# Two-layer diffusion backbone with gated DeltaNet: a pool of its own for the keys of heads 2 and 3, and the condition vectors loaded first

## The chip, the cores and the metric

The kernel runs on one core of one Trainium2 chip. The time is device microseconds of one launch, compared by the median over runs. Engines are named as in the profile: PE (TensorE), DVE (VectorE), ACT (ScalarE), POOL (GpSimd), SP (SyncE, which issues the DMAs).

## The reference, cut to what matters

Two layers, each with a mixing part and a ConvFFN, over 128 context tokens and 1024 latent tokens with 1024 features. The mixing part projects the normalized input once and gives its columns to three groups; the kernel treats the 1152 tokens together, as 9 tiles of 128.

```python
def mixing(h, lp, ctx):
    (a_val, a_gate, q_b, k_b, v_b, z_b, beta_raw, decay_raw,
     q_c, k_c, v_c) = split_projection(h @ lp['w_in'])
    o_a = conformer_conv(a_val, a_gate, ...)          # u = a_val * sigmoid(a_gate); depthwise conv width 31; LayerNorm; silu
    o_b, s_f, s_b = gated_deltanet(q_b, k_b, v_b, z_b, beta_raw, decay_raw, ...)
    o_c = neighbourhood_attention(q_c, k_c, v_c, ...) # or context_attention for the context tokens
    return jnp.concatenate([o_a, o_b, o_c], axis=-1) @ lp['w_out']
```

In `gated_deltanet` q, k and v go through a convolution of width 3 and a silu, and there are 4 heads. Each head is worked in chunks, forward and backward:

```python
    lmat = jnp.where(strict, jnp.einsum('bhnid,bhnjd->bhnij', kb, k) * decay, 0.0)
    sol = lax.linalg.triangular_solve(jnp.eye(CHUNK) + lmat, rhs, lower=True, unit_diagonal=True)
    ...
    s_final, o = lax.scan(step, s0, xs)               # one step for each chunk, a state of 128x128
```

`lmat` needs only k, beta and the decays. The condition vectors enter as `silu(cvec) @ w_ada + b_ada`; the decays of DeltaNet start from `exp(a_log)`.

## The kernel before

All matrix products of the projections are made of three products of high and low parts (L429 to L431, `mm3`), so that float32 precision is kept. A weight block of 128 columns is loaded as `raw` (two buffers), ACT makes `whi`, POOL makes `wlo = raw - whi` (L420). With it `dense` makes one step of 24 matmuls for each of three token blocks (384, 384, 385 columns).

In each layer the DeltaNet heads come in two pairs:

1. Heads 0 and 1: `gdn_dense` makes q, k, v. `preps` makes `lmat` for both, and `invert` (L1617) inverts all its 32x32 diagonal blocks at once, 72 blocks on 72 partitions: a load `F<-fd`, 30 pairs of DVE operations (L1627, L1628) of which each needs the one before, a store `fy<-F`. `gdn_blocks` loads the result back (`room<-fy`), transposes it (L813) and multiplies the blocks up to the full inverse on PE (L820, many small matmuls).
2. `gdn_scan`: the recurrence over the tiles for heads 0 and 1 (L930 to L970; its DVE rows write `ty`).
3. The list `STEPS` = k2, k3, c, q2, e, q3, e, v2, e, v, v3 orders what the program writes next. k2 and k3 are the keys of heads 2 and 3 (`gdn_piece` with `keep`: they stay in SBUF). c is the conformer's dense steps: gate and value blocks, with the DVE product `thg` of both. e is the next stage of `early`: first `gdn_early` for head 2, then for head 3 (turned keys, k·k products, `lmat`), then a second `invert`. v is the conformer's convolution (`conf_conv`): 8 chunks of 292 or 291 columns with 31 DVE operations each on `cu`, 248 a layer. The first `NCV` = 3 chunks are written at the step v, the other 5 (L1712) where the second pair's blocks are written.
4. Output of heads 0 and 1 (`z_dense`, `gdn_out`), then blocks and scan of heads 2 and 3, then attention, the output projection and the ConvFFN.

The order on each engine is not that of the program's text there: a scheduler with priorities sets it (`high_priority(-LOW)` puts the convolution behind, `high_priority(-LOWI)` the second inversion), from dependencies and a model of durations. An order written out by hand rules only the start, attention and the end of the FFN. So a buffer that comes free late moves all that hangs on it.

The buffers in question: pool `r0` (left side) holds `vT` of heads 0 and 1 and the 2880-column tile `F`/`room` of their inversion and blocks; it is given back after the blocks of heads 0 and 1. Pool `r2` comes later on the same side, so it takes the space that `r0` gives back. The tile `e` of `early` lies in `r2`: 3 x 1152 columns for the keys of heads 2 and 3 and for `DA`, and 256 for `kc`. A second `e` holds `F` and the temporary of the second inversion.

Of the kernel before, what the change touches and what calls it, by code (L numbers as in the profile page):

```python
# [9 lines left out]
F32 = mybir.dt.float32  # L10
# [10 lines left out]
KT = 8  # L21
NLAT = 1024
NT = 9
NTOK = 1152
# [19 lines left out]
FB = 2  # L44
ECOLS = 3 * NTOK + 256
NCV = 3
# [62 lines left out]
class K:  # L109
# [23 lines left out]
    def setup(self):  # L133
# [29 lines left out]
        o = VEC["ln_g"][0]  # L163
        nc.vector.tensor_scalar(out=self.hln, in0=vec[:, :, o:o + 4], scalar1=0.5, scalar2=None, op0=ALU.mult)
        self.al = cp.tile([128, L, 2, 2, H], F32, name="al")
        for l in range(L):
            for r in range(2):
                nc.sync.dma_start(out=self.al[:, l, :, r, :], in_=I["adt"][l:l + 1, :, r, :].to_broadcast([128, 2, H]))
            self.act(self.al[:, l, 0], self.al[:, l, 0], AF.Exp)
        cv = cp.tile([128, KT, 2], F32, name="cv")  # L170
        nc.sync.dma_start(out=cv, in_=I["cvec"])
        self.cs = cp.tile([128, KT, 2], F32, name="cs")
        self.act(self.cs, cv, AF.Silu)

# [493 lines left out]

    def gdn_early(self, l, h, S, pool, e, fd):

        nc = self.nc
        i = h - 2
        k = e[:, NTOK * i:NTOK * i + NTOK]
        DA = e[:, 2 * NTOK:3 * NTOK].rearrange("p (m f) -> p m f", f=128)
        kc = e[:, 3 * NTOK:ECOLS]
        nc.sync.dma_start(out=DA, in_=self.dec[i][1])
# [924 lines left out]

    def early(self, l, S, pool, rp):

        fd = self.dp.tile([72, 2, 32, 32], F32, tag="fd", name="fd", bufs=2)
        es = []
        e = rp.tile([128, ECOLS], F32, tag="e", name="e", bufs=1)
        yield e
        for h in (2, 3):
            es.append(self.gdn_early(l, h, S, pool, e, fd[:, h - 2]))
            yield  # L1610
        e = rp.tile([128, ECOLS], F32, tag="e", name="e", bufs=1)
        F = e[0:72, 0:2048].rearrange("p (i a b) -> p i a b", i=2, a=32)
        with self.tc.high_priority(-LOWI):
            w = self.invert(fd, F, e[0:72, 2048:])
        self.es = [(*x, w[:, i]) for i, x in enumerate(es)]
# [17 lines left out]
    def run(self):  # L1633
# [23 lines left out]
        for l in range(L):  # L1657
# [8 lines left out]
            with P("r0") as rp:  # L1666
                ds = [self.gdn_dense(l, h, hh, gc, hp[h], rp) for h in range(2)]
                for h in (2, 3):
                    E, tmp = (hp[h - 2].tile([128, NT, 128], F32, tag=t, name="E", bufs=1) for t in ("XN", "ktm"))
                    self.decays(h, S, E, tmp)  # L1670
                    nc.sync.dma_start(out=self.dec[h - 2][1], in_=E)
                heads = self.preps(l, ds, S, gc, hp, rp)
            sc = left.enter_context(P("scan"))
            o01 = self.gdn_scan(l, heads, S, sc)
            pcp = left.enter_context(P("pconv"))
            with P("r2") as rp:
                ea = self.early(l, S, gc, rp)
                ek = next(ea)
                for step in STEPS:
                    if step == "c":  # L1680
                        self.conf_dense(l, hh, gc)
                    elif step == "e":
                        next(ea, None)
                    elif step == "v":
                        with self.tc.high_priority(-LOW):
                            self.conf_conv(l, range(NCV), pcp)
                    else:
                        h = int(step[1])
                        keep = ek[:, NTOK * (h - 2):NTOK * (h - 1)] if step[0] == "k" else None
                        self.gdn_piece(l, h, "kqv".index(step[0]), hh, gc, keep)  # L1690
            for (h, X, _), o in zip(heads, o01):
                run(self.z_dense(l, h, hh, gc))
# [167 lines left out]
```

## Time and profile before

| | |
|---|---|
| median of 3 runs | 3556.93 us (3555.36 to 3557.3) |
| profiled execution | 3560.4 us |
| its span | 3558.6 us |
| busy: PE, DVE, ACT, POOL | 90%, 59%, 37%, 32% of the span |
| layer 0, first L813 / second L813 | 267.71 / 576.56 us |
| layer 1, first L813 / second L813 | 2056.77 / 2367.87 us |

Durations come from the profiled execution. In a timeline each row has its start and its duration in us, an "x" with the number of like instructions in a row, and in brackets how long the engine was idle ahead of it and what ended that. A window's row gives how long each engine was busy in that stretch; PEclk is the granted clock of TensorE as a share of its upper level (1.0 is 2.4 GHz, 0.5 is 1.2 GHz).

### The profile page before, as it was taken

The page shows a single profiled execution, that of the slowest core. Times are in us where ns is not written, and L with a number is a line of the kernel's source. Part 1 is how long each engine was busy: PE and PEld are TensorE (multiplying, and loading weights), DVE is VectorE, ACT ScalarE, POOL GpSimd, SP SyncE. Part 2 cuts the span into 40 slices and gives each one's busy share as a digit, 9 for nine tenths or more (in the row PEclk, how much of TensorE's full clock was granted, in tenths as well). Part 3 has the DMA queues.
Part 4 walks back from the last instruction along what each step waited for, and adds up shares of the span by engine and source line. Part 5 has one row for each costly group of instructions (what it writes and reads, how often), then busy time and mean ns, then how long its engine had stood idle before and what let it go on. Part 6 is the DMA issues. An engine that isn't in the chain of part 4 may idle for free.

```text
span 3558.6 us, 51089 instructions
## 1 busy us (share of the span) xinstructions
PE 3194.8 (90%) x19072; PEld 2883.6 (81%) x19072; DVE 2104.6 (59%) x3952; ACT 1327.9 (37%) x2988; POOL 1137.9 (32%) x1125
## 2 busy tenths in 40 slices
PE   7857888889999999999988668888799999999997
PEld 4857876755899988989978668787578999999997
DVE  3566896453566566656476758985644444444446
ACT  4425233463543333333254252335644222322223
POOL 2413312523444344434244132225333111221114
PEclk9988989999999999999999879898899999999999
DMA  5410353346423222222144113533452111111113
GB/s 184 113 50 28 112 171 116 94 125 196 133 86 97 70 78 86 81 69 78 42 137 128 42 38 100 160 110 79 127 166 85 41 36 39 45 53 43 36 36 130
DMA packets 243086, 323.79 MB, mean 91 GB/s; under 512 B 76175, under 2 KB 169631, under 8 KB 241750
## 3 DMA queue, kind: packets, MB, share of 16 engines
q1 hardware_dynamic: 242838, 320.52, 29.5%
q8 instruction: 151, 2.47, 0.3%
q14 instruction: 97, 0.79, 0.1%
HBM read 252.85 MB, written 67.59 MB: 90 GB/s over the span
## 4 chain that ended last, share of the span: by engine, by line
PE 58%; DVE 8%; DMA 3%; POOL 3%; ACT 2%; issue 2%; SPq 1%; DVEq 0%; POOLq 0%; ACTq 0%
PE d L429 17%; PE d L431 17%; PE d L430 17%; DVE cu L119 2%; DVE cv L119 1%; PE a L930 1%; POOL wlo L420 1%; PE d L600 1%; DVE adacc L119 1%; PE b L273 1%; POOL adacc L223 1%; DVE F L1628 0%; PE a L820 0%; PE a L387 0%; DVE XN L1627 0%
## 5 line engine op out<-in xcount | busy, mean ns | idle before, releaser
L431 PE MATMUL d<-hhi,wlo 128*128 128x386 f32 (+1 forms) x3072 | 1054.7, 343 | 17.5 <-POOL wlo L420 17.5
L429 PE MATMUL d<-hhi,whi 128*128 128x386 f32 (+1 forms) x3072 | 1051.7, 342 | 13.6 <-DVE cv L119 12.0
L430 PE MATMUL d<-hlo,whi 128*128 128x386 f32 (+1 forms) x3072 | 1051.5, 342 | 0.0
L420 POOL TENSOR_TENSOR wlo<-raw,whi 128x1024 fp32r<-128x1024 f32 x136 | 362.3, 2665 | 1112.2 <-ACT whi L116 1110.5
L429 PEld LDWEIGHTS d<-hhi,whi 128*128 128x128 f32 x3072 | 584.9, 190 | 19.3 <-issue 14.6
L431 PEld LDWEIGHTS d<-hhi,wlo 128*128 128x128 f32 x3072 | 583.0, 190 | 20.3 <-POOL wlo L420 19.1
L119 DVE SCALAR_TENSOR_TENSOR cv<-d,fvec,cv 128x384 f32<-128x384 f32 (+1 forms) x528 | 325.2, 617 | 463.6 <-ACT cv L116 455.1
L430 PEld LDWEIGHTS d<-hlo,whi 128*128 128x128 f32 x3072 | 585.2, 191 | 2.2 <-issue 0.7
L1539 DVE TENSOR_TENSOR f<-d,f 128x512 f32<-128x512 f32 x360 | 244.9, 686 | 164.2 <-PE d L431 162.3
L116 ACT ACTIVATE cv<-d,fvec 128x384 f32<-128x384 f32 (+1 forms) x264 | 174.7, 663 | 440.9 <-PE d L431 432.6
L429 PE MATMUL d<-wdh,ahi 128*128 128x512 f32 x792 | 315.6, 398 | 11.2 <-DVE f L1539 8.8
L430 PE MATMUL d<-wdl,ahi 128*128 128x512 f32 x792 | 313.4, 396 | 0.0
L431 PE MATMUL d<-wdh,alo 128*128 128x512 f32 x792 | 312.5, 395 | 0.0
L119 DVE SCALAR_TENSOR_TENSOR cu<-cu,vec 128x292 f32<-128x292 f32 (+1 forms) x480 | 257.3, 568 | 4.2
L116 ACT ACTIVATE whi<-raw 128x1024 fp32r<-128x1024 f32 x136 | 143.9, 1058 | 197.6 <-PE d L430 127.9
L223 POOL TENSOR_TENSOR adacc<-adacc,adpr 128x512 f32<-128x512 f32 x112 | 152.9, 1365 | 125.5 <-ACT adpr L116 97.5
L429 PEld LDWEIGHTS d<-wdh,ahi 128*128 128x128 f32 x792 | 148.9, 188 | 50.4 <-DVE f L1539 13.4
L431 PEld LDWEIGHTS d<-wdh,alo 128*128 128x128 f32 x792 | 148.7, 188 | 36.2 <-issue 0.7
L430 PEld LDWEIGHTS d<-wdl,ahi 128*128 128x128 f32 x792 | 148.8, 188 | 34.4 <-issue 1.4
L1526 POOL TENSOR_TENSOR wdl<-rawd,wdh 128x512 fp32r<-128x512 f32 x88 | 118.4, 1345 | 181.7 <-ACT wdh L116 181.1
L116 ACT ACTIVATE adpr<-adraw,cs 128x512 f32<-128x512 f32 x112 | 81.0, 723 | 240.0 <-POOL adacc L223 191.6
L1515 DVE TENSOR_TENSOR alo<-sg,ahi 128x384 fp32r<-128x384 f32 x132 | 111.9, 848 | 70.0 <-ACT ahi L116 69.8
(381 smaller groups left out, 5202.4 us busy)
## 6 DMA issues: line engine op xcount, KB each, us to landing
raw<-in_w_up_t SPq DMA_DIRECT2D x88, 512.0 KB
adraw<-in_w_ada SPq DMA_DIRECT2D x112, 256.0 KB
raw<-in_w_in_t SPq DMA_DIRECT2D x48, 512.0 KB
rawd<-in_w_down SPq DMA_DIRECT2D x88, 256.0 KB
xs<-x SPq DMA_DIRECT2D x27, 512.0 KB
x<-xs SPq DMA_DIRECT2D x27, 512.0 KB
rawa<-in_w_ada SPq DMA_DIRECT2D x24, 512.0 KB
x<-in_x SPq DMA_DIRECT2D x18, 512.0 KB
```

What stands on the lines that cost most here:

```text
L116: return self.nc.scalar.activation(out=out, in_=in_, func=func, **kw)
L119: return self.nc.vector.scalar_tensor_tensor(out=out, in0=in0, scalar=s, in1=in1, op0=op0, op1=op1, **kw)
L223: nc.gpsimd.tensor_tensor(out=acc[:, 1, :], in0=acc[:, 1, :], in1=pr, op=ALU.add)
L273: nc.tensor.matmul(ps[0:2, :], self.cs[:, k, :], r[:, 512 * i:512 * i + 512], start=(k == 0), stop=False)
L420: nc.gpsimd.tensor_tensor(out=lo[:, :n], in0=raw[:, :n], in1=hi[:, :n].bitcast(F32), op=ALU.subtract)
L429: nc.tensor.matmul(out, shi, mhi, start=(i == 0), stop=False)
L430: nc.tensor.matmul(out, shi, mlo, start=False, stop=False)
L431: nc.tensor.matmul(out, slo, mhi, start=False, stop=(i == n - 1))
L600: nc.tensor.matmul(ps[:, :NBC[b]], w[:, k, :], x[:, k, :NBC[b]], start=(k == 0 and i == 0), stop=(k == KT - 1 and i == 2))
L1515: nc.vector.tensor_tensor(out=lo[:, :n], in0=sg[:, :n], in1=hi[:, :n].bitcast(F32), op=ALU.subtract)
L1526: nc.gpsimd.tensor_tensor(out=lo, in0=raw[:, :512], in1=hi[:].bitcast(F32), op=ALU.subtract)
L1539: nc.vector.tensor_tensor(out=f[t][:, cs], in0=ps, in1=f[t][:, cs], op=ALU.add)
```

## The change

The keys of heads 2 and 3 get a tile `keys` of 2 x 1152 columns in a pool `keys` on the right side, opened when `r0` is closed in the program's text, and closed behind `r2`. The tile `e` shrinks to 1152 + 256 columns for `DA` and `kc` and is allocated once. The second inversion takes `F` from `keys` (the keys are used up by then) and its temporary from `e`. In `setup` the load of the condition vectors and their silu come ahead of the loads and exponentials of the decay factors.

```diff
-ECOLS = 3 * NTOK + 256
+ECOLS = NTOK + 256
...
+        cv = cp.tile([128, KT, 2], F32, name="cv")
+        nc.sync.dma_start(out=cv, in_=I["cvec"])
+        self.cs = cp.tile([128, KT, 2], F32, name="cs")
+        self.act(self.cs, cv, AF.Silu)
         self.al = cp.tile([128, L, 2, 2, H], F32, name="al")
...
-        cv = cp.tile([128, KT, 2], F32, name="cv")
-        nc.sync.dma_start(out=cv, in_=I["cvec"])
-        self.cs = cp.tile([128, KT, 2], F32, name="cs")
-        self.act(self.cs, cv, AF.Silu)
...
-    def gdn_early(self, l, h, S, pool, e, fd):
+    def gdn_early(self, l, h, S, pool, keys, e, fd):
...
-        k = e[:, NTOK * i:NTOK * i + NTOK]
-        DA = e[:, 2 * NTOK:3 * NTOK].rearrange("p (m f) -> p m f", f=128)
-        kc = e[:, 3 * NTOK:ECOLS]
+        k = keys[:, NTOK * i:NTOK * i + NTOK]
+        DA = e[:, 0:NTOK].rearrange("p (m f) -> p m f", f=128)
+        kc = e[:, NTOK:ECOLS]
...
-    def early(self, l, S, pool, rp):
+    def early(self, l, S, pool, keys, rp):
...
         e = rp.tile([128, ECOLS], F32, tag="e", name="e", bufs=1)
-        yield e
         for h in (2, 3):
-            es.append(self.gdn_early(l, h, S, pool, e, fd[:, h - 2]))
+            es.append(self.gdn_early(l, h, S, pool, keys, e, fd[:, h - 2]))
             yield
-        e = rp.tile([128, ECOLS], F32, tag="e", name="e", bufs=1)
-        F = e[0:72, 0:2048].rearrange("p (i a b) -> p i a b", i=2, a=32)
+        F = keys[0:72, 0:2048].rearrange("p (i a b) -> p i a b", i=2, a=32)
         with self.tc.high_priority(-LOWI):
-            w = self.invert(fd, F, e[0:72, 2048:])
+            w = self.invert(fd, F, e[0:72])
...
+            ks = ExitStack()
+            keys = ks.enter_context(R("keys")).tile([128, 2 * NTOK], F32, name="keys", bufs=1)
             sc = left.enter_context(P("scan"))
...
-                        keep = ek[:, NTOK * (h - 2):NTOK * (h - 1)] if step[0] == "k" else None
+                        keep = keys[:, NTOK * (h - 2):NTOK * (h - 1)] if step[0] == "k" else None
...
+            ks.close()
```

PE, layer 0, before: around the first block product (names: d is the accumulator of a dense step, a that of the blocks).

```order
L430 MATMUL d_3086<-hlo_144,whi_3082 128x386
L431 MATMUL d_3086<-hhi_143,wlo_3083 128x386
L820 MATMUL a_1864<-room_1821,DA_1557 32x32 x36
L820 MATMUL a_1902<-room_1821,DA_1601 32x32 x2
L820 MATMUL a_1940<-room_1821 32x32 x25
L820 MATMUL a_1902<-room_1821,DA_1601 32x32 x34
L820 MATMUL a_1940<-room_1821 32x32 x11
L820 MATMUL a_1941<-room_1821 32x32 x18
```

PE, layer 0, after, around its first block product; d_3086 is called d_3088 there.

```order
L429 MATMUL d_3404<-hhi_149,whi_3346 128x388
L430 MATMUL d_3404<-hlo_150,whi_3346 128x388
L431 MATMUL d_3404<-hhi_149,wlo_3347 128x388
L429 MATMUL d_3404<-hhi_149,whi_3346 128x388
L430 MATMUL d_3404<-hlo_150,whi_3346 128x388
L820 MATMUL a_1864<-room_1821,DA_1557 32x32 x2
L431 MATMUL d_3404<-hhi_149,wlo_3347 128x388
L429 MATMUL d_3404<-hhi_149,whi_3346 128x388
```

Behind d_3086/d_3088, the first conformer step, eleven further dense steps (d_3115 to d_3404) now stand ahead of, or around, the first block product. The rest of the last of them and the steps of head 2's query stand between the block products.

DVE, layer 0, before: in the middle of the first inversion (XN is its temporary).

```order
L1627 TENSOR_TENSOR XN_1559<-F_1755 72x476
L1628 TENSOR_TENSOR F_1755<-F_1755,XN_1559 72x2x14x17
L1627 TENSOR_TENSOR XN_1559<-F_1755 72x468
L1628 TENSOR_TENSOR F_1755<-F_1755,XN_1559 72x2x13x18
L1627 TENSOR_TENSOR XN_1559<-F_1755 72x456
L1628 TENSOR_TENSOR F_1755<-F_1755,XN_1559 72x2x12x19
L1627 TENSOR_TENSOR XN_1559<-F_1755 72x440
L1628 TENSOR_TENSOR F_1755<-F_1755,XN_1559 72x2x11x20
```

DVE, layer 0, after, the same place; thg is the conformer's gate, d its value.

```order
L1626 TENSOR_TENSOR F_1755<-F_1755,XN_1559 72x2x15x16
L1625 TENSOR_TENSOR XN_1559<-F_1755 72x476
L119 SCALAR_TENSOR_TENSOR thg_3113<-thg_3113,d_3175 128x384
L1626 TENSOR_TENSOR F_1755<-F_1755,XN_1559 72x2x14x17
L1625 TENSOR_TENSOR XN_1559<-F_1755 72x468
L1626 TENSOR_TENSOR F_1755<-F_1755,XN_1559 72x2x13x18
L1625 TENSOR_TENSOR XN_1559<-F_1755 72x456
L1626 TENSOR_TENSOR F_1755<-F_1755,XN_1559 72x2x12x19
L1625 TENSOR_TENSOR XN_1559<-F_1755 72x440
L119 SCALAR_TENSOR_TENSOR thg_3140<-thg_3140,d_3202 128x384
L1626 TENSOR_TENSOR F_1755<-F_1755,XN_1559 72x2x11x20
```

Two (and later a third) products of the conformer's gate have come into the chain. Ahead of these rows stand all eight writes `keys<-th,cv` and the convolution operations of head 3's key, five of them behind the inversion's first operation; before, `e<-th,cv` stood behind the block products.

DVE, layer 0, before: end of the second inversion (cu is the convolution's accumulator, room the blocks' tile).

```order
L119 SCALAR_TENSOR_TENSOR cu_5578<-cu_5577,vec_79,cu_5578 128x291
L1627 TENSOR_TENSOR e_3930<-e_3930 72x60
L119 SCALAR_TENSOR_TENSOR cu_5578<-cu_5577,vec_79,cu_5578 128x291
L1628 TENSOR_TENSOR e_3930<-e_3930 72x2x30
L119 SCALAR_TENSOR_TENSOR cu_5578<-cu_5577,vec_79,cu_5578 128x291 x26
L813 STREAM_TRANSPOSE room_4519<-room_4519 32x576 x4
L815 TENSOR_TENSOR XN_4521<-room_4519 32x9x32 x4
L794 COPY room_4519<-a_4610 128x288
L813 STREAM_TRANSPOSE room_4519<-room_4519 32x576 x4
```

DVE, layer 0, after, from just ahead of the second pair's first L813.

```order
L119 SCALAR_TENSOR_TENSOR cu_5477<-cu_5476,vec_79,cu_5477 128x292
L119 SCALAR_TENSOR_TENSOR cu_5512<-cu_5511,vec_79,cu_5512 128x292
L119 SCALAR_TENSOR_TENSOR cu_5477<-cu_5476,vec_79,cu_5477 128x292
L119 SCALAR_TENSOR_TENSOR cu_5512<-cu_5511,vec_79,cu_5512 128x292
L813 STREAM_TRANSPOSE room_4523<-room_4523 32x576 x4
L815 TENSOR_TENSOR XN_4525<-room_4523 32x9x32 x4
L119 SCALAR_TENSOR_TENSOR cu_5477<-cu_5476,vec_79,cu_5477 128x292
L794 COPY room_4523<-a_4614 128x288
L119 SCALAR_TENSOR_TENSOR cu_5512<-cu_5511,vec_79,cu_5512 128x292 x4
L813 STREAM_TRANSPOSE room_4523<-room_4523 32x576 x4
L815 TENSOR_TENSOR XN_4532<-room_4523 32x9x32 x4
L794 COPY XN_4525<-a_4690 32x9x32
```

Before, all 248 convolution operations of the layer stand ahead of this L813. After, 172 do, and 76 stand behind it, between the block products (188 and 60 in layer 1).

## Rows read from the trace of the kernel before

**Rows 1.** Page, part 1: busy time, share and instructions by engine.

```profile
PE 3194.8 (90%) x19072; PEld 2883.6 (81%) x19072; DVE 2104.6 (59%) x3952; ACT 1327.9 (37%) x2988; POOL 1137.9 (32%) x1125
```

**Rows 2.** List of PE's waits: total us, times, longest.

```profile
PE a L820 <- DVE room L813: 87.5, 8, 39.8
PE d L317 <- DMA rawa<-in_w_ada: 18.2, 1, 18.2
PE d L431 <- POOL wlo L420: 17.5, 5, 7.2
```

**Rows 3.** Timeline of PE: start, duration, operation, [idle before, releaser].

```profile
229.47 0.34 PE L430 MATMUL d<-hlo,whi 128*128 128x386 f32 x1
229.64 0.34 PE L431 MATMUL d<-hhi,wlo 128*128 128x386 f32 x1
268.53 0.39 PE L820 MATMUL a<-room,DA 32*32 32x32 f32 x4 [38.54 <-DVE room L813]
2057.59 0.39 PE L820 MATMUL a<-room,DA 32*32 32x32 f32 x4 [39.78 <-DVE room L813]
```

**Rows 4.** Timeline of DVE, first inversion of layer 0.

```profile
223.26 0.27 DVE L1627 TENSOR_TENSOR XN<-F 72x60 f32<-72x60 f32 x1 [7.42 <-DMA F<-fd]
242.90 0.65 DVE L1627 TENSOR_TENSOR XN<-F 72x476 f32<-72x476 f32 x1
250.70 0.54 DVE L1627 TENSOR_TENSOR XN<-F 72x368 f32<-72x368 f32 x1
257.27 0.22 DVE L1628 TENSOR_TENSOR F<-F,XN 72x60 f32<-72x60 f32 x1
267.71 3.17 DVE L813 STREAM_TRANSPOSE room<-room 32x576 f32<-32x576 f32 x4 [10.22 <-DMA room<-fy]
```

**Rows 5.** Windows, layer 0: PE, PEld, DVE, ACT, POOL busy; PEclk; DMA share; GB/s.

```profile
223.00:268.00 45.00, 6.99 (x40) 6.65 (x38) 32.42 (x61) 1.35 (x2) 4.88 (x5) 0.63 0.16 38
268.00:306.00 38.00, 21.10 (x542) 18.56 (x543) 20.18 (x49) 21.39 (x79) 2.59 (x4) 0.68 0.08 24
306.00:360.00 54.00, 53.29 (x398) 49.77 (x397) 37.27 (x129) 33.72 (x128) 30.83 (x64) 0.99 0.12 44
360.00:577.00 217.00, 183.31 (x982) 177.48 (x981) 199.85 (x410) 59.14 (x145) 53.94 (x27) 0.89 0.44 131
577.00:649.00 72.00, 68.58 (x773) 49.82 (x771) 24.42 (x50) 31.75 (x98) 10.96 (x15) 0.95 0.39 122
```

**Rows 6.** Windows, layer 1.

```profile
2057.00:2368.00 311.00, 259.62 (x1922) 247.42 (x1923) 255.83 (x586) 114.73 (x352) 87.70 (x92) 0.87 0.34 102
2368.00:2420.00 52.00, 49.90 (x735) 45.25 (x733) 27.74 (x49) 30.84 (x97) 12.97 (x17) 1.00 0.30 88
```

**Rows 7.** Timeline of DVE, end of the second inversion, layer 0.

```profile
559.07 0.51 DVE L119 SCALAR_TENSOR_TENSOR cu<-cu,vec 128x291 f32<-128x291 f32 x1
559.50 0.20 DVE L1627 TENSOR_TENSOR e<-e 72x60 f32<-72x60 f32 x1
560.19 16.45 DVE L119 SCALAR_TENSOR_TENSOR cu<-cu,vec 128x291 f32<-128x291 f32 x26
576.56 3.16 DVE L813 STREAM_TRANSPOSE room<-room 32x576 f32<-32x576 f32 x4
```

**Rows 8.** Timeline of DVE, a write of head 2's key, layer 0.

```profile
304.65 0.55 DVE L119 SCALAR_TENSOR_TENSOR e<-th,cv 128x384 f32<-128x384 f32 x1
```

**Rows 9.** Timelines of POOL and DVE, the same stretch.

```profile
226.78 2.47 POOL L420 TENSOR_TENSOR wlo<-raw,whi 128x1024 fp32r<-128x1024 f32 x1 [3.37 <-ACT whi L116]
227.03 2.56 DVE L1627 TENSOR_TENSOR XN<-F 72x300 f32<-72x300 f32 x1
229.62 0.47 DVE L1628 TENSOR_TENSOR F<-F,XN 72x300 f32<-72x300 f32 x1
```

**Rows 10.** Timeline of ACT, start of the kernel.

```profile
13.06 1.28 ACT L116 ACT_TABLE_LOAD   x1
14.35 0.21 ACT L116 ACTIVATE cs<-cv 128x16 f32<-128x16 f32 x1
```

More of the change, by code (lines that the diff above doesn't have):

```diff
@@ L1676, in run @@
             with P("r2") as rp:
-                ea = self.early(l, S, gc, rp)
-                ek = next(ea)
+                ea = self.early(l, S, gc, keys, rp)
                 for step in STEPS:
```

## The prediction

> **What bounds the kernel now.** I read the busy shares first, then the list of waits, then the timelines of the engines at the longest wait, then the windows by stage. The row of the busy shares says that TensorE (PE) is busy 90% of the span [rows 1], so a gain has to come out of its idle time or its slow clock. The reader should look in the list of waits for the one entry that is large and happens rarely: PE's first block products (L820) wait 87.5 us in 8 waits for VectorE's (DVE's) transposes L813 [rows 2]. In the timeline of PE, two of the eight are nearly all of it: 38.54 us in layer 0, 39.78 in layer 1 [rows 3]. In each, DVE runs the first 32-wide inversion, from 223.26 to about 257.5, and then waits 10.22 us for the result to go through memory and back [rows 4]. PE has no instruction to do until then, and the granted clock sinks: 0.63 in that stage and still 0.68 in the next one [rows 5].
>
> The windows cut layer 0 at the first inversion, the block products, the scan of heads 0 and 1, the long stretch up to the second L813 (with the second inversion in it), and the block products up to the scan of heads 2 and 3 [rows 5]; for layer 1 the middle three stand as one [rows 6]. Take what lies between the first L813 and the second. In layer 0 it lasts 309 us; DVE is busy 20.2 + 37.3 + 199.9 = 257.4 of it, and PE 21.1 + 53.3 + 183.3 = 257.7. In layer 1 it is 311 us, DVE 255.8, PE 259.6. Both engines stand at 83%, but not at once: DVE is idle in the blocks and the scan, and from 360 to 577 it is busy for 199.9 of 217 us (92%), PE for 183.3. The last 26 conv operations run 16.45 us with no gap to the second L813 behind them [rows 7], so there the conv work itself sets the end.
>
> **The change, part by part.** The decisive part is that keys of heads 2 and 3 no longer wait for room that the first heads' preparation gives back. In the trace they are written at 304.65, in the stage after the first blocks [rows 8]. In the new order they are written ahead of and inside the first inversion, the key convolutions free their buffers, and PE gets 11 more dense steps ahead of the first L820. A dense step is 24 matmuls, which start 0.177 us apart [rows 3], so 4.2 us; 11 of them hold 264 matmuls, of which 248 stand before the first block product: 43.6 us of PE work that fills the 38.5 us gap.
>
> *In the first inversion.* DVE gets 19 more operations ahead of L813: 8 writes of keys, 6 convolution operations of head 3's key, 5 products of the conformer's gate. The row of one shows 0.55 us [rows 8]; an operation shown with 0.51 us lets the next start after 0.43 [rows 7], so I take 0.5 us from start to start: 9.5 us. Nine stand ahead of the inversion, in the 7.42 us in which DVE waits for its load [rows 4], and two behind it, in the 10.22 us of the way through memory. The other 8 lie in the serial chain: 4 us. They can also make it wait, because a gate product needs PE's dense step. Head 3's key ends one step ahead of PE's 229.8, at 225.6; three gate steps and one value step later the first product can run, at 242.5, the others one step (4.2 us) apart, at 246.7 and 250.9. DVE comes to the first and the last behind the operations that now start at 242.90 and 250.70 [rows 4], each later by the serial ones ahead of it, so at about 246 and 254. I take 0 for waits; the other end is the longest wait of PE for prepared weights, 7.2 us [rows 2], three times.
>
> Every dense piece (3 steps, 12.7 us) also needs one POOL operation on its weights. Here the trace shows a price. While the one at 226.78 ran (2.47 us), the inversion's 72x300 operation took 2.56 us; its twin right behind it took 0.47 [rows 9]. So one costs 2.1 us of the chain. At one per 12.7 us two more fall into the inversion: 4.2 us. The Trainium skill (SBUF — State Buffer, section "Who interferes with whom") says that a DVE instruction with two SBUF inputs contends with a GpSimd instruction that reads SBUF, and that the loser is fully blocked. By that rule it speaks against the change, because the conversions move from a time with mixed work into a serial chain; the trace agrees with 2.56 beside 0.47 us. By a reading of the row as a chance outlier the sum would be 4.2 us per layer better.
>
> So the first L813 comes 8 us later (0 at best, 30 with all three waits).
>
> *Between the two L813.* Ahead of it went the 9.5 us above. In the new order only 172 of the 248 conv operations are ahead of the second L813 in layer 0 (188 in layer 1), where all 248 were before. One starts 0.43 us ahead of what follows it, or takes 0.63 as the mean of the last 26 (16.45 us) [rows 7]. I take 0.43, since what lengthens the 26 is not taken along by the moved ones: 76 and 60 of them take 32.7 and 25.8 us (47.9 and 37.8 at 0.63). DVE's work falls to 257.4 − 9.5 − 32.7 = 215.2, and 220.5 in layer 1; PE's to 257.7 − 43.6 = 214.1, and 216.0. How long the stretch lasts depends on how much of it both engines fill. If the share stays 83%, it is 259 and 266 us. If it is that of the stretch from 360 on, 92%, it is 234 and 240. The new order puts about 25 conv operations (10.8 us) into the scan, and second-query work into the blocks on PE and DVE, which had 17.8 and 16.7 us of idle DVE; that speaks for more than 83%. Against the upper end: the recurrence of the scan and the blocks still alternate between engines. I take 87%: 247 and 253.5 us, so 62 and 57.5 us less. (The ends give 50 and 45, or 75 and 71.)
>
> *Behind the second L813.* The conv operations left over join a stage of 72 us in which DVE has 24.4 busy, and in layer 1 one of 52 us with 27.7 [rows 5, 6]. In layer 0 57 fit into 72, PE being busy 68.6 there, so they are hidden except where one stands in front of a block copy: I take 5 us (0 to 32.7). In layer 1 53.5 do not fit into 52: 10 us (1.5 to 25.8).
>
> *Queues.* On SyncE the store of the second head's finished key now stands ahead of the inversion's load. That key's dense steps end about 213 (two pieces and one step ahead of 229.6 make 12.7 + 4.2), and its last write some 4 us behind; the load's data is there at 223.2 now [rows 4]. I take 0, with 2 us at most. Weight loads now stand ahead of the inversion's result; the DMA engines are 16% busy in that stage, so they do not delay it.
>
> *Conditions loaded first.* The silu of the condition vectors now comes ahead of the exponentials. One table load of 1.28 us, at 13.06, is moved to a later place; the silu follows it at 14.35 [rows 10]. The first product waits for a weight load until 18.2 us [rows 2]. What is gained hides behind that load: 0.
>
> **Sum.** Layer 0: −62 + 8 + 5 = −49. Layer 1: −57.5 + 8 + 10 = −39.5. Together −88.5 us, against the profiled execution's 3560.4 (a span of 3558.6 and 1.8 around it): 3472. The median of the runs is 3556.93, 3.5 lower, and on that scale the forecast is 3468.
>
> **Rivals.**
> A, more: both engines fill the middle to 92%, and POOL and the tail cost nothing. 75 + 71 − 8 (the serial operations, 4 per layer) = 138 less: 3419. For it: the fast stretch has that share already, and PE's clock need not sink. Against: the blocks and the scan stay chains.
> B, less: the share stays 83% and the scan is drawn out by what is put into it; 50 + 45 − 16 − 15, and some 7 us for one wait in each inversion: 50 less, 3507. For it: both engines work in order, and the new order ties them more closely.
> C, no difference: the order says that the keys are early, but the inversion of heads 2 and 3 starts no sooner because its DMAs and conv operations in front hold it, and PE's filled gap comes back as a wait later: 3557. Against: 76 conv operations are really gone from in front of it, and the tail behind that inversion had no gap.
> D, slower: the first inversion waits three times for the gate products (3 × 7.2, plus 8: 30 us per layer), and the conv operations behind the second L813 stand in the chain of block products in full (32.7 and 25.8). At an 83% share that is 50 − 62.6 = −12.6 and 45 − 55.8 = −10.8: 23 us longer, 3580. It decides as soon as these waits exceed the 50 and 45 us won. For it: DVE has nothing else while it waits for PE; against: the gate products are due later than their dense steps end.
>
> **How the numbers follow.** Forecast (75 to 110 less and around, 3440 to 3490) 0.56, A 0.13, B 0.21, C 0.04, D 0.06. About 0.2% (7 us) is what a measurement of this kernel tells from no change. Faster is the forecast, A and B: 0.90; same 0.04; slower 0.06. The range takes A's end and B's, with a little beyond B for dearer waits: 3420 to 3520.
>
> **What the new profile would show.** Right: the wait of L820 for L813 falls from 38.5 and 39.8 to a few us and the clock in the first inversion stays at its upper level (1.0 in place of 0.63); the inversion has 72-wide operations of about 2.5 us at two more places; the first L813 is about 8 us later; the second L813 of layer 0 about 54 us sooner (at 523), with conv operations behind it. The middle's share is read from the same windows. Wrong: if DVE's rows in the first inversion show idle time ended by PE, B or D holds; if the second L813 comes sooner but the scan of heads 2 and 3 does not, the conv operations moved behind it are on the path; if L820 still waits for tens of us, C.

## The result, and the profile after

The changed kernel takes 3429.57 us (median of 4 runs, 3426.76 to 3437.32) against 3556.14 us of the kernel before on the same chip: a ratio of 0.9649, 95% interval 0.9632 to 0.9666. That is 127 us less (3556.14 − 3429.57), where 88.5 were forecast; 3468 was the figure and 3420 to 3520 the range. The sign, the place and the filled gap were as told; the size was too small by some 30%. One execution of the run with the conversions on DVE in the kernel before (4061.55 us, at a granted clock of 0.735 where the others have about 0.95) fell into the chip's slow state and is left out below.

PE's busy time and its list of waits, to be held against [rows 1, 2]: the busy share goes up while the busy time falls by only 12 us, so what is gone is idle time and, at most for those 12 us, slow clock.

```profile
PE 3182.8 (93%) x19072; PEld 2874.3 (84%) x19072; DVE 2094.5 (61%) x3952; ACT 1323.0 (39%) x2987; POOL 1151.5 (34%) x1125
```

```profile
PE a L820 <- DVE room L813: 18.3, 9, 5.3
...
PE d L431 <- POOL wlo L420: 14.9, 5, 5.1
```

PE's timeline at the first block product of each layer (start, duration, operation, idle before and what ended it). Where [rows 3] had waits of 38.54 and 39.78 us, about 2 us remain of each:

```profile
276.20 0.32 PE L820 MATMUL a<-room,DA 32*32 32x32 f32 x4 [2.06 <-DVE room L813]
...
1992.99 0.32 PE L820 MATMUL a<-room,DA 32*32 32x32 f32 x4 [2.46 <-DVE room L813]
```

DVE's timeline through the first inversion of layer 0, and POOL's under it, to be held against [rows 4, 9]. The lines 1627 and 1628 are 1625 and 1626 now.

```profile
224.07 0.26 DVE L1625 TENSOR_TENSOR XN<-F 72x60 f32<-72x60 f32 x1 [0.41 <-DMA F<-fd]
...
227.33 2.52 DVE L1625 TENSOR_TENSOR XN<-F 72x260 f32<-72x260 f32 x1
...
240.42 2.75 DVE L1626 TENSOR_TENSOR F<-F,XN 72x468 f32<-72x468 f32 x1
...
247.90 0.54 DVE L119 SCALAR_TENSOR_TENSOR thg<-thg,d 128x384 f32<-128x384 f32 x1
...
252.25 0.54 DVE L119 SCALAR_TENSOR_TENSOR thg<-thg,d 128x384 f32<-128x384 f32 x1
252.71 2.69 DVE L1626 TENSOR_TENSOR F<-F,XN 72x440 f32<-72x440 f32 x1
...
258.35 0.55 DVE L119 SCALAR_TENSOR_TENSOR thg<-thg,d 128x385 f32<-128x385 f32 x1
...
264.81 0.22 DVE L1626 TENSOR_TENSOR F<-F,XN 72x60 f32<-72x60 f32 x1
268.58 0.55 DVE L119 SCALAR_TENSOR_TENSOR thg<-thg,d 128x384 f32<-128x384 f32 x1 [3.56 <-PE d L431]
272.82 0.55 DVE L119 SCALAR_TENSOR_TENSOR thg<-thg,d 128x384 f32<-128x384 f32 x1 [3.69 <-DMA room<-fy]
275.38 3.17 DVE L813 STREAM_TRANSPOSE room<-room 32x576 f32<-32x576 f32 x4 [2.00 <-DMA us<-thg]
```

```profile
227.04 2.52 POOL L420 TENSOR_TENSOR wlo<-raw,whi 128x1024 fp32r<-128x1024 f32 x1 [2.81 <-ACT whi L116]
239.79 2.88 POOL L420 TENSOR_TENSOR wlo<-raw,whi 128x1024 fp32r<-128x1024 f32 x1 [10.22 <-ACT whi L116]
252.53 2.40 POOL L420 TENSOR_TENSOR wlo<-raw,whi 128x1024 fp32r<-128x1024 f32 x1 [9.86 <-ACT whi L116]
```

The reader should see four things. The nine operations ahead of the inversion fit into the old wait for its load (0.41 us is left of 7.42). The three gate products in the chain (247.90, 252.25, 258.35) do not wait; the two behind it (268.58, 272.82) do, the first of them for PE, but inside the way through memory, which takes hardly longer than before: 10.35 us from the chain's end to L813, 10.22 before. There are long rows at two more places, each beside a POOL row, one per 12.7 us, as the forecast placed them. And L813 comes at 275.38, 7.7 us later than before; 8 were forecast.

The windows, cut at the same events as [rows 5, 6] (PE, PEld, DVE, ACT, POOL busy; PEclk; DMA share; GB/s), five of layer 0 and three of layer 1:

```profile
224.00:275.40 51.40, 50.14 (x284) 49.80 (x282) 40.26 (x71) 8.17 (x14) 12.63 (x8) 1.00 0.30 86
275.40:319.20 43.80, 36.50 (x638) 31.62 (x638) 24.42 (x55) 26.21 (x89) 6.45 (x6) 0.91 0.19 55
319.20:375.00 55.80, 55.05 (x411) 52.16 (x411) 48.06 (x156) 35.46 (x144) 34.32 (x67) 0.98 0.23 76
375.00:510.80 135.80, 115.91 (x631) 111.94 (x630) 129.96 (x281) 41.75 (x103) 35.69 (x19) 0.91 0.52 156
510.80:583.20 72.40, 67.99 (x766) 49.57 (x765) 63.39 (x125) 32.08 (x98) 19.98 (x15) 0.95 0.41 123
...
1941.10:1992.20 51.10, 49.44 (x280) 49.10 (x278) 39.97 (x71) 7.89 (x13) 12.80 (x8) 1.00 0.31 85
1992.20:2229.50 237.30, 209.34 (x1681) 197.13 (x1682) 201.26 (x491) 103.53 (x335) 77.63 (x89) 0.92 0.39 117
2229.50:2289.60 60.10, 50.97 (x726) 45.47 (x724) 56.78 (x109) 31.81 (x98) 23.36 (x17) 0.94 0.29 81
```

PE is busy through the whole first inversion, at the upper clock level (1.00, where it was 0.63). The stretch from the first L813 to the second is 235.4 us in layer 0 (309 before) and 237.3 in layer 1 (311 before): 73.5 and 73.8 us less. In the last stage DVE has 63.4 us of work in place of 24.4, in the same 72 us.

### The profile page after: what moved, and what is told of

Read it like the earlier page. It is cut to its first block, busy times and chain, and to the rows that moved or that the text cites. A ratio compares the mean times of both kernels' runs of the same rounds, so it can differ in the third digit from the quotient of the medians.

```text
span 3426.6 us, 51062 instructions
## 1 busy us (share of the span) xinstructions
PE 3182.8 (93%) x19072; PEld 2874.3 (84%) x19072; DVE 2094.5 (61%) x3952; ACT 1323.0 (39%) x2987; POOL 1151.5 (34%) x1125
## 4 chain that ended last, share of the span: by engine, by line
PE 59%; DVE 8%; DMA 4%; POOL 3%; issue 2%; ACT 2%; SPq 1%; DVEq 0%; POOLq 0%; ACTq 0%
PE d L429 18%; PE d L431 18%; PE d L430 18%; DVE cu L119 1%; PE a L930 1%; DVE adacc L119 1%; PE a L387 1%; DVE cv L119 1%; DVE XN L1625 1%; PE b L273 1%; DVE F L1626 0%; PE a L820 0%; PE S L1307 0%; PE c L241 0%; DVE keys L1626 0%
## 5 line engine op out<-in xcount | busy, mean ns | idle before, releaser
L431 PE MATMUL d<-hhi,wlo 128*128 128x386 f32 (+1 forms) x3072 | 1059.0, 345 | 14.9 <-POOL wlo L420 14.9
L429 PE MATMUL d<-hhi,whi 128*128 128x386 f32 (+1 forms) x3072 | 1055.3, 344 | 6.4 <-DVE cv L119 6.4
L420 POOL TENSOR_TENSOR wlo<-raw,whi 128x1024 fp32r<-128x1024 f32 x136 | 348.7, 2566 | 1064.7 <-ACT whi L116 1063.1
L431 PEld LDWEIGHTS d<-hhi,wlo 128*128 128x128 f32 x3072 | 585.6, 191 | 17.9 <-POOL wlo L420 16.4
L429 PEld LDWEIGHTS d<-hhi,whi 128*128 128x128 f32 x3072 | 587.6, 191 | 10.7 <-issue 8.8
L429 PE MATMUL d<-wdh,ahi 128*128 128x512 f32 x792 | 315.6, 398 | 10.9 <-DVE f L1539 8.4
L431 PE MATMUL d<-wdh,alo 128*128 128x512 f32 x792 | 312.5, 395 | 0.0
L119 DVE SCALAR_TENSOR_TENSOR cu<-cu,vec 128x292 f32<-128x292 f32 (+1 forms) x480 | 248.2, 559 | 1.9
L429 PEld LDWEIGHTS d<-wdh,ahi 128*128 128x128 f32 x792 | 149.0, 188 | 50.0 <-DVE f L1539 13.1
L431 PEld LDWEIGHTS d<-wdh,alo 128*128 128x128 f32 x792 | 148.7, 188 | 36.1 <-issue 0.7
```

What stands on the lines that cost most here:

```text
L119: return self.nc.vector.scalar_tensor_tensor(out=out, in0=in0, scalar=s, in1=in1, op0=op0, op1=op1, **kw)
L420: nc.gpsimd.tensor_tensor(out=lo[:, :n], in0=raw[:, :n], in1=hi[:, :n].bitcast(F32), op=ALU.subtract)
L429: nc.tensor.matmul(out, shi, mhi, start=(i == 0), stop=False)
L431: nc.tensor.matmul(out, slo, mhi, start=False, stop=(i == n - 1))
```

## The experiments

Each is compared with the kernel before on its own chip, by the ratio; the changed kernel's is 0.9649 (0.9632 to 0.9666).

**Which half of the change.** Two runs take it apart. The first is the changed kernel with the old setup order, by the edit below; the second is the kernel before with the same lines moved the other way.

```diff
-        cv = cp.tile([128, KT, 2], F32, name="cv")
-        nc.sync.dma_start(out=cv, in_=I["cvec"])
-        self.cs = cp.tile([128, KT, 2], F32, name="cs")
-        self.act(self.cs, cv, AF.Silu)
         self.al = cp.tile([128, L, 2, 2, H], F32, name="al")
...
             self.act(self.al[:, l, 0], self.al[:, l, 0], AF.Exp)
+        cv = cp.tile([128, KT, 2], F32, name="cv")
+        nc.sync.dma_start(out=cv, in_=I["cvec"])
+        self.cs = cp.tile([128, KT, 2], F32, name="cs")
+        self.act(self.cs, cv, AF.Silu)
```

> The changed kernel with the old order in the setup (decay factors first, condition vectors behind them); the pool of the keys alone is changed. Theory 1 (all of the gain is from the keys' own room): the same as the changed kernel within 5 us, so 3425 to 3437 us. Theory 2 (the setup order has a part, since the condition vectors start the first products): slower than the changed kernel by 3 to 10 us.

> The kernel before with only the setup reordered. Theory 1: no difference, 3553 to 3559 us, because the first product waits for its weights till 18.2 us in any case. Theory 2: 1 to 3 us faster, by the table load that is moved.

The pool alone: 0.966 (0.9638 to 0.9683), 3435.68 us. The setup alone: 1.0012 (1.0000 to 1.0023), 3560.62 beside 3557.91 us. The intervals of the first and of the whole change lie over each other, and the second shows no gain. So all that can be measured comes from the pool.

**Is it the filled gap, or the early keys?** Here the keys stay in the room that comes free late; only the order of writing is changed, so that the conformer fills the gap (an edit of the kernel before):

```diff
-STEPS = ("k2", "k3", "c", "q2", "e", "q3", "e", "v2", "e", "v", "v3")
+STEPS = ("c", "k2", "k3", "q2", "e", "q3", "e", "v2", "e", "v", "v3")
```

> The kernel before, with the keys still in the room that is given back late, but with the conformer's dense steps written ahead of the keys of heads 2 and 3, so that PE has work in the first inversion that needs no late room. Theory A (any independent dense work in that gap does it, and the DVE work spreads as a consequence): the wait of PE for L813 goes from 87.5 us to below 25 and the time to 3425 to 3460. Theory C (the early keys are needed, since the second inversion hangs on them): the gap is filled, but the second inversion starts less than 20 us sooner per layer: 3500 to 3540.

0.9721 (0.9701 to 0.9741), 3456.6 us: by the ratio 99 us less than before (0.0279 x 3557.91), where the change gives 125 (0.0351 x 3557.91). A row of PE's waits and the windows of layer 0, for the first inversion and for the middle:

```profile
PE a L820 <- DVE room L813: 15.6, 6, 4.8
```

```profile
222.70:274.20 51.50, 47.56 (x269) 47.22 (x267) 41.44 (x70) 8.08 (x12) 12.44 (x8) 0.99 0.29 73
274.20:525.60 251.40, 216.27 (x1696) 204.03 (x1696) 209.41 (x504) 107.60 (x342) 76.46 (x91) 0.90 0.37 114
```

Theory A holds for four fifths of the gain: any independent dense work in that gap does it, without a byte of new room. The wait is gone as with the pool, and PE's clock stays at its upper level (0.99). The trace of this run also has 172 convolution operations ahead of the second L813 and 76 behind it, as the changed kernel has. So it shows that the new room is not needed for most of the gain; what the filled gap would bring without that shift it does not show. The remaining fifth goes theory C's way: the second inversion starts 166.9 us behind the first L813 and not 153.0, and the middle is 251 and not 235 us long. It can't be read from that stage alone, since other work is shifted too: the scan of heads 2 and 3 starts 345.3 us behind the first inversion's start (359.2 in the changed kernel), and layer 1's inversion follows 1393 us behind that (1358).

The same order in the changed kernel (below), and in a second run the conformer between the two keys (k2, c, k3, q2, and so on):

```diff
-STEPS = ("k2", "k3", "c", "q2", "e", "q3", "e", "v2", "e", "v", "v3")
+STEPS = ("c", "k2", "k3", "q2", "e", "q3", "e", "v2", "e", "v", "v3")
```

> The changed kernel, with the conformer's dense steps written ahead of the keys of heads 2 and 3 as in the run on the old room. The gap is then filled with either; the keys come some 50 us later but still in their own room. Theory A (only that the gap is filled counts): as the changed kernel, 3425 to 3440. Theory C (early keys bring the second inversion forward): slower by 10 to 30 us, as far as the second inversion starts later, between 428 and 441 us: 3440 to 3457.

> The changed kernel with the conformer's dense steps written between the keys of head 2 and head 3. The gap is filled either way. Theory A (only that the gap is filled counts): as the changed kernel, 3425 to 3440. Theory C (early keys): between the changed kernel and the one with the conformer first, 5 to 15 us slower.

0.9675 (0.9656 to 0.9694) and 0.9669 (0.9650 to 0.9688), 3439.56 and 3438.06 us. Both lie a little above the changed kernel, and their intervals and its own overlap: nothing more than a leaning to theory C can be read. Against the run before, the same order gains half a per cent (0.9721 to 0.9675, the intervals apart) when the keys have their own room.

**The convolution operations that moved behind the second L813.** The scheduler left 76 of them there. Two priorities in the changed kernel bring all 248 ahead of it again:

```diff
-LOW, LOWI = 3000, 500
+LOW, LOWI = -300, 4000
```

> The changed kernel with two priorities altered so that all 248 convolution operations of a layer stand ahead of the second pair's first L813 again, as before the change, where the changed kernel has 172; some 32 us of dense work on PE is drawn ahead of it with them. Theory A (DVE's work ahead of the second L813 sets when it comes): 76 x 0.43 = 33 us more at a share of 0.86 to 0.93, so 35 to 38 us later per layer, and given back behind it only what the tail has lost (0.3 us in layer 0, 8.7 in layer 1): 55 to 65 us slower than the changed kernel, 3485 to 3495. Theory B (PE's filled gap is what counts; PE has other dense work to do meanwhile): at most 15 us slower, 3430 to 3445.

0.9928 (0.9909 to 0.9948), 3530.4 us: by the ratios 99 us slower than the changed kernel (0.0279 x 3557.91), worse than either theory. Layer 1 is spoiled by another queue. SyncE's and DVE's timelines there:

```profile
2336.20 5.51 SPq L1164 DMA_DIRECT2D RB<-in_rpb  x16
2341.81 0.32 SPq L1628 DMA_DIRECT2D fy<-keys  x1
```

```profile
2310.64 0.38 DVE L1626 TENSOR_TENSOR keys<-keys,e 72x60 f32<-72x60 f32 x1
2352.08 3.17 DVE L813 STREAM_TRANSPOSE room<-room 32x576 f32<-32x576 f32 x4 [41.07 <-POOL room L810]
```

The inversion ends at 2311.0, but its store is issued at 2341.8, behind the attention's loads of keys, values and biases on the in-order SyncE: 31 us that no theory here speaks of. Layer 0 has no such wait. From the first inversion to the scan of heads 2 and 3 it takes 384.0 us (224.09 to 608.08) beside 359.2: 25 us more. The second L813 comes 62 us later (572.77 for 510.75), but 180 matmuls of dense steps (L429 to L431 and L600) that stood behind it now stand ahead, 32 us at 0.177, and the stage behind it is 37 us shorter. Layer 1 takes 415.7 us (1972.73 to 2388.39) beside 348.4: 67 us more, 36 without the 31. So the two layers make 61 us without the queue's wait, in theory A's 55 to 65, but not as theory A has them: it gives some 36 us to layer 0 and 28 to layer 1, so the agreement of the sum is in part luck. That the 31 us would have been nothing without the queue is argued, not shown. Theory B's 15 us are passed by layer 0 alone. The edit also puts the second inversion itself further back: in layer 0 the last convolution operation starts at 531.54, and the inversion runs on until 558.16, where in the kernel before the convolution ended last, at the L813. So the 25 us of layer 0, of the 66 that it had gained, are the price of both priorities together.

The gap is still filled in this run (275.41 − 224.09 = 51.3 us from the first inversion to L813, as in the changed kernel), and yet only 26 us of the gain are left (0.0072 x 3557.91), 57 if the 31 us are taken off. The filled gap and the order of DVE's work behind it are not two sums that add up.

The opposite direction in the changed kernel, still fewer ahead of it:

```diff
-LOW, LOWI = 3000, 500
+LOW, LOWI = 3000, 0
```

> The changed kernel with the second inversion at the common priority (500 steps higher), so that 154 in place of 172 convolution operations stand ahead of the second L813 and 217 in place of 248 ahead of the second scan. Theory A (DVE's work ahead of the second L813 sets it): 18 x 0.43 = 7.7 us sooner there per layer, given back behind it where DVE is the busier: 0 to 10 us faster, 3420 to 3430. Theory B (what is left is bound by PE): no difference, or 5 us slower by the convolution that ends later.

0.9679 (0.9657 to 0.9702), 3441.74 us: no gain, rather a loss, with intervals that overlap. In layer 0 the second L813 comes 284.5 us behind the first inversion's start, 2.2 sooner, and the scan of heads 2 and 3 363.6 us behind it, 4.4 later. Theory A's sign is refuted, and theory B (no difference, or some 5 us slower) is the nearer. In layer 1 the second scan comes 3.3 us sooner (345.2 us behind the first inversion, 348.4 in the changed kernel). Most of the loss lies behind that scan: 1147.7 us to the end beside 1137.1, where 31 convolution operations were still to be done in place of 16.

**What a convolution operation costs in the crowd.** The forecast took 0.43 us. In the groups of DVE by shape, between the two L813 of layer 0, before and after:

```profile
L119 DVE SCALAR_TENSOR_TENSOR cu<-cu,vec 128x292 f32<-128x292 f32 x180 | 94.9, 552 | 1.0
L119 DVE SCALAR_TENSOR_TENSOR cu<-cu,vec 128x291 f32<-128x291 f32 x60 | 37.3, 621 | 1.1
```

```profile
L119 DVE SCALAR_TENSOR_TENSOR cu<-cu,vec 128x292 f32<-128x292 f32 x136 | 70.2, 554 | 0.3
L119 DVE SCALAR_TENSOR_TENSOR cu<-cu,vec 128x291 f32<-128x291 f32 x30 | 15.5, 516 | 0.0
```

74 rows fewer take 132.2 − 85.7 = 46.5 us with them: 0.63 us each, the upper end of the forecast's bounds. Neighbouring rows overlap a little in these sums; counted without the overlap, all 76 operations (these 74 and the first steps of two chunks) take 44.0 us with them, 0.58 each. The mean of the 240 rows before was 0.55 (132.2 / 240), so it was dear rows that went. Two kinds of them can be seen in the timelines of POOL and DVE before:

```profile
395.64 2.62 POOL L420 TENSOR_TENSOR wlo<-raw,whi 128x1024 fp32r<-128x1024 f32 x1 [4.33 <-ACT whi L116]
```

```profile
395.92 2.66 DVE L119 SCALAR_TENSOR_TENSOR cu<-cu,vec 128x292 f32<-128x292 f32 x1
...
566.86 0.52 DVE L119 SCALAR_TENSOR_TENSOR cu<-cu,vec 128x291 f32<-128x291 f32 x1
567.42 0.52 DVE L119 SCALAR_TENSOR_TENSOR cu<-cu,vec 128x291 f32<-128x291 f32 x1
```

The first kind lies beside a conversion on POOL: six rows in layer 0, 13.5 us together, and in the changed kernel two, 4.2 us. The second kind stands in a run in which each operation needs the accumulator of the one before: such rows start 0.56 us apart, where the others start 0.43 apart. There are 56 of them before and 9 after. The last 26 of [rows 7] are such a run. No conversion lies beside them, since POOL's last one ends at 559.0; only their last three rows (1.04, 1.57 and 0.95 us) stand beside POOL's masks for the blocks (L808, L810). So the 0.63 us of [rows 7] was not the price of the conversions.

To see what POOL's conversions do, they are made on DVE in the kernel before (in `gdn_dense`, `gdn_piece` and `conf_dense`, which pass `eng=self.nc.vector`):

```diff
-    def weight(self, src, cols=128, kt=KT):
+    def weight(self, src, cols=128, kt=KT, eng=None):
...
-        nc.gpsimd.tensor_tensor(out=lo[:, :n], in0=raw[:, :n], in1=hi[:, :n].bitcast(F32), op=ALU.subtract)
+        (eng or nc.gpsimd).tensor_tensor(out=lo[:, :n], in0=raw[:, :n], in1=hi[:, :n].bitcast(F32), op=ALU.subtract)
```

> The kernel before, with the low part of the weights of heads' q, k, v and of the conformer made on DVE in place of POOL; 234 in place of 248 convolution operations are then ahead of the second L813. Theory A (each conversion on POOL costs the convolution on DVE some 2 us, so that a convolution operation in the crowded stretch costs 0.62 and not 0.43 us): the convolution operations there show 0.50 to 0.52 us in the mean, those behind the second inversion start 0.43 us apart, and the time is 10 to 35 us less, 3520 to 3546. Theory B (the long rows are not POOL's doing): the mean stays at 0.55 to 0.62, DVE has 12 x 1.2 us more in that stretch, and the time is 10 to 30 us more, 3566 to 3586.

0.9952 (0.9936 to 0.9969), 3538.74 us: 17 us less, as theory A said. DVE's timeline at the end of the second inversion, and the groups by shape:

```profile
549.17 14.81 DVE L119 SCALAR_TENSOR_TENSOR cu<-cu,vec 128x292 f32<-128x292 f32 x34
...
556.97 0.52 DVE L119 SCALAR_TENSOR_TENSOR cu<-cu,vec 128x292 f32<-128x292 f32 x1
557.40 0.52 DVE L119 SCALAR_TENSOR_TENSOR cu<-cu,vec 128x291 f32<-128x291 f32 x1
```

```profile
L119 DVE SCALAR_TENSOR_TENSOR cu<-cu,vec 128x292 f32<-128x292 f32 x180 | 91.1, 535 | 0.2
L119 DVE SCALAR_TENSOR_TENSOR cu<-cu,vec 128x291 f32<-128x291 f32 x47 | 24.3, 517 | 0.5
```

34 operations take 14.81 us, 0.44 each, where 26 took 16.45 in [rows 7]. That came as theory A said, but not for its reason: here rows of two chunks (292 and 291 columns) stand in turn, so that none needs the one just before it. What does bear on theory A is the count of rows beside a conversion: six became two in the middle of each layer, both beside conversions that the edit leaves on POOL (`z_dense` and `attn_dense`). The mean of a row falls to 0.517 to 0.535 us, not quite to the 0.50 to 0.52 of the expectation. The 17 us are not the price of the conversions in the middle alone: 5.6 of the 20.7 us between the two spans lie ahead of the first inversion (217.70 for 223.26), and 14 convolution operations moved behind the second L813.

**The same in the changed kernel**, with all of these on DVE; then without the conformer's; then with all of them again and head 2's query ahead of the conformer (`STEPS` = k2, k3, q2, c, ...):

> The changed kernel with the low part of the weights of heads' q, k, v and of the conformer made on DVE in place of POOL. No weight conversion is then on POOL beside the first inversion. Theory A (a conversion on POOL holds a DVE operation with two inputs in SBUF for some 2.1 us, three times in the first inversion): no 72-wide operation above 1 us is left there; the conversion itself takes 1.2 us on DVE by the 1.36 us of the 128x1152 product L657, so the first inversion to the first L813 is 51.3 - 6.5 + 3.6 = 48.4 us, and the kernel is 5 to 20 us faster than the changed one, 3410 to 3425. Theory B (the 2.5 us rows are something else, such as a DMA): rows of 2.5 us stay in the inversion, DVE has the conversions on top, and the kernel is 5 to 30 us slower, 3435 to 3460.

> The changed kernel with the low parts of q, k, v on DVE, but those of the conformer on POOL, so that five gate products and not six stand ahead of the first L813. Theory A (the wait for the sixth product is what took the gain of the run with all on DVE): the first L813 is as early as in the changed kernel, the crowded stretch is freed of collisions, and the time is 5 to 15 us less than the changed kernel's, 3415 to 3425. Theory B (what is left is bound by PE): 3425 to 3435.

> The changed kernel with all these low parts on DVE and head 2's query written ahead of the conformer, so that four gate products stand ahead of the first L813 and the last of them sooner. Theory A (the gate products ahead of L813 hold it): the first L813 comes at 268 to 272 us and the time is 5 to 15 us less than the changed kernel's. Theory B (bound by PE): 3425 to 3440.

0.9647 (0.9629 to 0.9666), 0.9650 (0.9633 to 0.9666) and 0.9663 (0.9643 to 0.9683): 3429.99, 3434.31 and 3435.69 us, none different from the changed kernel. DVE's timeline of the first of them:

```profile
235.81 1.22 DVE L420 TENSOR_TENSOR wlo<-raw,whi 128x1024 fp32r<-128x1024 f32 x1
...
264.39 0.56 DVE L119 SCALAR_TENSOR_TENSOR thg<-thg,d 128x384 f32<-128x384 f32 x1 [2.06 <-PE d L431]
268.63 0.56 DVE L119 SCALAR_TENSOR_TENSOR thg<-thg,d 128x384 f32<-128x384 f32 x1 [3.69 <-PE d L431]
272.94 0.56 DVE L119 SCALAR_TENSOR_TENSOR thg<-thg,d 128x385 f32<-128x385 f32 x1 [3.75 <-PE d L431]
...
274.94 3.16 DVE L813 STREAM_TRANSPOSE room<-room 32x576 f32<-32x576 f32 x4
```

The mechanism is theory A's: a conversion takes 1.22 us on DVE and no other row above 1 us is left in the inversion. But from its start to L813 it takes 54.3 us (220.66 to 274.94), not 48.4, because the place of the long rows is taken by a new wait: three gate products that need PE's dense steps stand ahead of L813 on the in-order DVE. The blocks' tile is ready at 271.27 (the end of POOL's mask L810), and L813 starts 3.7 us later. The two repairs did not bring it sooner either: L813 comes at 274.96 in the one, and in the last at 278.63 and not at 268 to 272. With PE at 93% of the span there is probably little left for such a shift to find; no run shows that this is the reason. No run beat the changed kernel.

## Why the prediction was right, and where its size was off

Step by step, layer 0 and layer 1, forecast beside measured:

| step | forecast | measured |
|---|---|---|
| first inversion to first L813 | +8, +8 | +6.9, +6.0 |
| first L813 to second | −62, −57.5 | −73.5, −73.8 |
| second L813 to the second scan | +5, +10 | +0.3, +8.7 |
| all else | 0 | −6.5 |

The sum of the measured column is the spans' difference, 132 us (3558.6 − 3426.6). The median differs by 127, since the profiled execution of before (3560.4 us) was longer than the median of its runs.

*The filled gap: right.* Eleven dense steps went into it, the wait fell from 87.5 to 18.3 us, and the run with the conformer first shows that other work in the gap, without the new room, brings about 100 us.

*The conversions in the chain: right in price and number.* Two more, at 240.42 and 252.71 us, at 2.1 us each (2.75 and 2.69 us shown, where the twin of each, the inversion's operation just ahead, takes 0.64 and 0.61). The eight other operations in the chain were priced too high: the chain is 6.7 us longer, of which these two make 4.2, so 0.3 us each and not 0.5.

*The share: right.* 87% was taken for the middle. Of 235.4 us PE is busy 36.5 + 55.1 + 115.9 = 207.5 (88%), DVE 24.4 + 48.1 + 130.0 = 202.5 (86%).

*DVE's work in the middle: the term that was mis-sized.* "I take 0.43, since what lengthens the 26 is not taken along by the moved ones" was wrong. The forecast left 215.2 us of work there and 202.5 were measured; in layer 1 220.5 and 201.3. The 76 operations took 44.0 us with them in place of 32.7, and the 11.3 between them are most of the 12.7 that were missing in layer 0. Dear rows did leave: those beside a conversion went from six to two (12 conversions on POOL stood in the middle of layer 0 before, 9 after), which is 13.5 − 4.2 − 4 x 0.43 = 7.6 us, and those in a run on one accumulator from 56 to 9, which is about 4 us (47 x 0.09, a row of 0.52 in place of 0.43). The first of the two is borne out by the run of the kernel before with the conversions on DVE; the second is read from the traces, and no run was made for it. The reading of [rows 7] as a price that the moved operations do not share was where this went astray: the 26 were long mostly because each needs the one before it. With 44.0, divided by the measured 0.86, the sum gives (257.4 − 9.5 − 44.0) / 0.86 = 237 us, where 235.4 were measured.

*The count in layer 1: a slip.* 60 operations were taken to be behind the second L813, 188 ahead; 60 are those ahead of the scan, and 16 more follow in it. It is 172 ahead and 76 behind in both layers, at 0.58 us another 9 us (16 x 0.58) for layer 1.

*The tail: too dear in layer 0.* 5 us were taken and 0.3 measured; DVE went from 24.4 to 63.4 of 72 us there at no cost. In layer 1, where there was no room, 8.7 of the 10 came.

*Rivals.* A had the time (3419, ten below the measured) by a share of 92% that did not come; its condition was not met. B, C and D are refuted by the middle's 73.5 us and by gate products that do not wait in the chain. The forecast's sign of being wrong, idle time of DVE ended by PE, does appear at 268.58 behind the chain, but it holds up nothing there; only in runs with the conversions on DVE does such a wait stand in front of a ready L813.

What stays open: the 6.5 us outside the three stages (5.0 gained between the second scan of layer 0 and layer 1's inversion, 2.3 behind the last, 0.8 lost ahead of the first). One profile of each kernel does not tell them from the spread of single runs, and no run was aimed at them.

## What to carry to other kernels

When an engine waits for a serial chain elsewhere, ask first what independent work is held back by a buffer, and whether writing other independent work sooner does the same: here a changed list of steps gave four fifths of what the new buffer gave. Price work that leaves a crowded stretch by what it costs in that stretch, not by its price alone, and look whether the rows that give a price need each other's results; price what joins a stage by that stage's idle time. Before work is moved on an in-order engine, look at what it will stand in front of: the wait taken out of the inversion came back as a wait for a gate product, and convolutions brought forward put an inversion's store behind 31 us of loads.

## What the runs showed of the hardware

A conversion on POOL and a DVE operation with both inputs in SBUF shut each other out, in both directions. A DVE row beside it mostly grows to 2.2 to 2.75 us. But where DVE issues such operations without a pause, POOL's own row grows from 2.4 us, and PE can be the one that waits. The timelines of POOL and DVE in the kernel before, and one of PE's waits in the same stage:

```profile
382.85 8.46 POOL L420 TENSOR_TENSOR wlo<-raw,whi 128x1024 fp32r<-128x1024 f32 x1 [10.07 <-ACT whi L116]
...
546.54 9.92 POOL L420 TENSOR_TENSOR wlo<-raw,whi 128x1024 fp32r<-128x1024 f32 x1 [23.87 <-ACT whi L116]
```

```profile
380.73 8.31 DVE L119 SCALAR_TENSOR_TENSOR cu<-cu,vec 128x292 f32<-128x292 f32 x19
388.96 0.55 DVE L119 SCALAR_TENSOR_TENSOR thg<-thg,d 128x384 f32<-128x384 f32 x1
```

```profile
556.51 0.69 PE L431 MATMUL d<-hhi,wlo 128*128 128x386 f32 x1 [6.43 <-POOL wlo L420]
```

The Trainium skill (SBUF — State Buffer, section "Who interferes with whom") says that whoever issues first has the port for the whole instruction. The DVE rows of 2.2 to 2.75 us agree with that. The POOL row of 8.46 us does not come out of it: 14 convolution operations began and ended after its start. It ends 2.35 us (391.31 − 388.96) after the start of the gate product, whose second input comes from PE's accumulator and not from SBUF, and its twin in layer 1 (9.08 us at 2173.43) 2.34 us after its own gate product. So in these two rows POOL got its turn when such an operation broke DVE's run; what let it in where it took 9.92 us (the row that PE waits for at 556.51), no run shows.

Two convolution operations in a row start 0.43 us apart on DVE when they work on different accumulators (556.97 and 557.40 above), and 0.56 us apart when the second needs the result of the first (566.86 and 567.42).

On DVE the conversion takes 1.22 us, half of POOL's 2.4, and moving it there was worth 17 us to the kernel before and nothing to the changed one.
